# Closing two units at a time, border steps at other times, and a mask in two operations

## The chip, the cores and the metric

One core of a Trainium2 chip runs the whole kernel in one launch. The metric is the time of one launch on the device in microseconds (us), the median of the runs. The engines are named as in the profile: PE is TensorE (PEld its weight loads), DVE is VectorE, ACT is ScalarE, POOL is GpSimd, SP is SyncE, which issues the DMAs.

## What is computed

One decoder layer on x of 1024 tokens by 1024 columns, in float32. One projection feeds two attention groups: a sparse one (8 heads of 64), in which an indexer scores the causal keys and each query keeps its 256 best, and a differential one (4 heads of 128). Their outputs are joined and projected, then an MLP follows; each half has a norm before and after.

```python
def block(i):                     # differential attention, per 128 queries
    p = probs(q1, k1f) - lam * probs(q2, k2f)
    o = jnp.einsum('bhqs,bshe->bqhe', p, vf)
...
o_d = (rmsnorm(o_d, g_diff_sub[layer]).astype(f32) * (1.0 - lam_init)).astype(x.dtype)
...
_, sel = lax.top_k(score, topk)   # sparse attention: 256 keys of each query
...
mix = jnp.concatenate([o_a.reshape(B, S, DSA_W), o_d.reshape(B, S, DIFF_W)], axis=-1)
y = jnp.einsum('bsc,cd->bsd', mix, w_out[layer])
x = x + rmsnorm(y, g_post_mix[layer])
h = rmsnorm(x, g_pre_mlp[layer])
u = jax.nn.relu(jnp.einsum('bsd,df->bsf', h, w_up[layer]))
y = jnp.einsum('bsf,fd->bsd', u * u, w_down[layer])
x = x + rmsnorm(y, g_post_mlp[layer])
```

## The kernel before

Tokens lie in 8 blocks of 128. A float32 factor of a product is split into a high part (a copy in the format fp32r, mostly by ACT) and a low part (the difference, mostly by DVE), and a product is three passes over them; names with `hl`, `hi`, `lo` or a last index 0 and 1 are such parts. The stages, by the trace's time:

- 0 to 200 us: projections of v, of the indexer and its scores (`idx_unit`, tile `si`).
- 200 to some 511: differential attention. A unit is one head and one block, 32 in all. `diff_A` computes both softmaxes (L622 adds the mask and takes the maximum on DVE, L624 the exponential on ACT) and joins them, p = p0 + p1 * st (L671). `diff_groups` transposes p and multiplies it by v into the PSUM bank `od`. `diff_end` (L707 to L716) closes a unit: ACT copies one half of `od` scaled by the reciprocal sum (L710), DVE scales the other half and adds it (L711), ACT squares, POOL takes the root (L103, L106), DVE scales by the root and by g_sub (L715), and a DMA writes the 128x128 result to `mb_d`. Between units PE runs pieces of the projections still due (`pj`, `pv_j`). Beside this runs the search of the 256th score, 31 rounds in two groups of three blocks: ACT counts signs (L523) and DVE one block's (L520), POOL compares (L525, L527), DVE sets bits (L528). At its end `topk_mask1` and `topk_mask2` make a mask of each of six blocks: `te` is 1 where a score is at the threshold, `tu` counts these along the row (L554), and three operations (L564 to L566) join sign and count. Here a scheduler sets the order on the engines; `tc.issue_after` ties steps of the search to units.
- some 473 to 670: sparse attention with these masks as the additive term of its softmax. `outB_load` (L846 to L850) reads `mb_d`, transposes it and splits it for the part of the output projection that is made here (`yb`, L868).
- 670 to 741: the rest of the output projection (`ya`, L1061) and, block by block, both norms (`block`). `load_wo(0)` loads four weight tiles through `split_w` into the two buffers of the tag `wst`.
- 741 to 1071: MLP up, in passes p of seven products P1 to P7 over sums and differences of operand quarters, as `up_mm` (L1023) runs them. `up_weights` makes the weights' sums (`su`) and splits, `mlp_up` adds the products up (`e1`, `e2`, `e3`, `u1`, `u2`), takes relu and square (L1186, L1187), makes sums again (`sd`, L1281 to L1286) and stores parts (`stg`).
- 1071 to 1351: MLP down, units (chunk c, quarter q) of seven products of six matmuls (`down_mm`, L1391); ACT or DVE moves each product to `yu` and `yq` (L1422, L1424). Then `last_unit`, four times, with the last norm (L1516 to L1535).

From 670 on all five engines' orders are written out: every step is put into a list by `do(t, step)` with a due time t in us, and the list is sorted by it. Due times are counted from the start of the block stage: `E` is the end of the last block's products, `U0` is E + 13 (the first pass's reference), `OPEN` E + 14.3, `D0` the start of the down products; `end[p, "P3"]` is a product's planned end, MM = 0.229 a planned matmul. An engine takes its steps in this order, so a step that waits holds all that stand behind it on its engine.

## Time and profile before

| | |
|---|---|
| runs | 1413.58, 1413.93, 1414.21 us; median 1413.93 |
| the profiled execution | 1407.41 us, its span 1405.6 us |
| PE | 1305.7 us busy, 93% of the span, 6520 matmuls |
| DVE | 1113.6 us, 79% |
| ACT | 748.0 us, 53% |
| POOL | 381.3 us, 27% |

Busy times are shares of the whole span and mix stages with different limits; a stretch's own row says which engine is near full there. In rows of single instructions the first number is the start, the second the duration, and the bracket at the end tells how long the engine was idle before it and whose end it waited for. PEclk is the clock that was granted to TensorE, as a share of its full one; on 2.4 GHz as 1.00, 0.50 is 1.2 GHz.

### The profile page before, as it was taken

What the parts mean: (1) busy time and instruction counts of PE and PEld (TensorE: products, weight loads), DVE (VectorE), ACT (ScalarE), POOL (GpSimd) and SP (SyncE); (2) the same over time, 40 slices, a digit from 0 to 9 for tenths busy, and PEclk for the clock granted to TensorE, in tenths of its full rate; (3) what the DMA queues carried; (4) which work ended last, traced back from release to release, by engine and by line L of the source; (5) the groups of instructions that cost most, each with busy time, mean ns of one, the idle gap of its engine ahead of it and who ended that gap; (6) DMA issues with size and microseconds to landing.
All of it is one profiled execution on the core that took longest, in us unless ns stands there. A gap on an engine that the chain in (4) does not pass through costs nothing.

```text
span 1405.6 us, 19947 instructions
## 1 busy us (share of the span) xinstructions
PE 1305.7 (93%) x6520; PEld 1094.3 (78%) x6520; DVE 1113.6 (79%) x2020; ACT 748.0 (53%) x1435; POOL 381.3 (27%) x559
## 2 busy tenths in 40 slices
PE   8999978999998879999788799999998999999997
PEld 8888857778886758888566688888887888888885
DVE  5538969898898888887698788888887578878666
ACT  5305538988974468887454566666666421112112
POOL 5477654775565243332120000000000000000002
PEclk9999998999998979999899899999999999999999
DMA  8766344465554465431661476766778776767646
GB/s 328 257 180 193 108 134 108 130 176 160 157 155 123 118 188 151 137 106 55 230 216 45 165 262 246 255 234 244 254 267 287 261 243 236 261 213 267 224 175 214
DMA packets 152169, 272.89 MB, mean 194 GB/s; under 512 B 15105, under 2 KB 83841, under 8 KB 152065
## 3 DMA queue, kind: packets, MB, share of 16 engines
q1 hardware_dynamic: 152064, 271.61, 58.8%
q8 instruction: 52, 0.85, 0.3%
q14 instruction: 53, 0.43, 0.1%
HBM read 172.46 MB, written 99.09 MB: 193 GB/s over the span
## 4 chain that ended last, share of the span: by engine, by line
PE 60%; DVE 16%; ACT 8%; issue 6%; POOL 5%; DMA 4%; SPq 0%; POOLq 0%; DVEq 0%; ACTq 0%
PE qab L1391 10%; PE pab L1023 8%; PE pj L166 7%; PE qc L1391 6%; PE qd L1391 6%; PE pc L1023 5%; PE pd L1023 5%; PE sa L621 2%; PE pv_j L252 2%; ACT jk L523 2%; PE v L354 2%; PE yb L868 2%; PE oa L825 1%; PE pta L811 1%; DMA v_d_d<-vt 1%
## 5 line engine op out<-in xcount | busy, mean ns | idle before, releaser
L166 PE MATMUL pj<-hT,w_whl 128*128 128x512 f32 (+1 forms) x960 | 226.7, 386 | 4.4 <-DVE vt L230 1.2
L166 PEld LDWEIGHTS pj<-hT,w_whl 128*128 128x128 f32 x960 | 173.7, 190 | 38.4 <-DVE vt L230 1.5
L1527 POOL TENSOR_TENSOR sq<-ss 128x1 f32<-128x1 f32 x8 | 5.6, 699 | 636.8 <-ACT jk L1520 636.8
L523 ACT ACTIVATE jk<-score,vbits 128x768 bf16<-128x768 f32 (+1 forms) x124 | 121.9, 983 | 16.0 <-DVE vbits L528 12.9
L624 ACT ACTIVATE p<-p,st 128x512 f32<-128x512 f32 (+7 forms) x108 | 84.7, 785 | 22.8 <-DVE st L622 18.1
L1023 PE MATMUL pab<-HB,w_up 128*128 128x512 f32 x384 | 92.9, 392 | 0.0
L1023 PEld LDWEIGHTS pab<-HB,w_up 128*128 128x128 f32 x384 | 72.1, 188 | 15.7
L868 PE MATMUL yb<-wo,mbhl 128*128 128x512 f32 x192 | 77.6, 436 | 0.6 <-ACT mbhl L849 0.5
L252 PE MATMUL pv_j<-w_whl,hT 128*128 128x256 f32 x576 | 73.0, 288 | 1.0 <-DVE fm L556 1.0
L252 PEld LDWEIGHTS pv_j<-w_whl,hT 128*128 128x128 f32 x576 | 71.6, 198 | 1.4 <-PE sa L621 1.1
L974 ACT ACTIVATE w_up<-su 128x1024 fp32r<-128x1024 f32 x32 | 33.7, 1052 | 63.1 <-DVE su L1008 59.8
L817 DVE TENSOR_TENSOR ptahl<-pta,ptahl 128x512 fp32r<-128x512 f32 (+2 forms) x112 | 55.4, 495 | 10.7 <-ACT ptahl L816 8.5
L474 DVE SCALAR_TENSOR_TENSOR score<-rl,wsgn,score 128x512 f32<-128x512 f32 (+5 forms) x42 | 54.8, 1305 | 11.0 <-ACT rl L470 8.7
L470 ACT ACTIVATE rl<-si,wabs 128x512 f32<-128x512 f32 (+5 forms) x48 | 40.4, 847 | 43.1 <-PE si L468 33.5
L793 POOL TENSOR_SCALAR p<-p,st 128x128 f32<-128x128 f32 (+7 forms) x60 | 46.8, 784 | 56.5 <-DVE st L792 55.1
L816 ACT ACTIVATE ptahl<-pta 128x512 fp32r<-128x512 f32 (+2 forms) x112 | 49.1, 441 | 22.2 <-PE pta L811 19.1
L1061 PE MATMUL ya<-wo,mixA 128*128 128x512 f32 x192 | 51.8, 426 | 9.8 <-ACT wo L111 4.6
L212 POOL TENSOR_TENSOR mm<-mm 128x512 f32<-128x512 f32 (+1 forms) x40 | 52.6, 1323 | 25.7 <-DVE mm L193 14.5
L1023 PE MATMUL pc<-HT,w_a 128*128 128x512 f32 x192 | 48.9, 406 | 7.8 <-DVE e L1238 7.8
L825 PE MATMUL oa<-ptahl,Va 128*128 128x256 f32 x320 | 53.1, 289 | 3.1 <-DVE ptahl L817 3.0
L621 PE MATMUL sa<-Kd,Qd 128*128 128x512 f32 (+4 forms) x192 | 46.8, 372 | 9.4 <-DVE st L622 9.4
L825 PEld LDWEIGHTS oa<-ptahl,Va 128*128 128x128 f32 x320 | 46.1, 189 | 12.0 <-DVE ptahl L817 4.7
(247 smaller groups left out, 3446.1 us busy)
## 6 DMA issues: line engine op xcount, KB each, us to landing
ul<-u_d SPq DMA_DIRECT2D x56, 896.0 KB, 6.1
u_d<-stg SPq DMA_DIRECT2D x184, 256.0 KB, 2.8
...
```

What stands on the lines that cost most here:

```text
L166: T.matmul(p[:m, :t1 - t0], wv[pw][:, kt, :m], hTs(ph, kt, t0, t1), start=(kt == 0 and j == 0), stop=(kt == KT - 1 and j == 2))
L212: G.tensor_tensor(o, o, mm[half][:, 1, :n], op=op)
L252: T.matmul(p[:, j2 * 256:(j2 + 1) * 256], hTs(ph, kt, tb * P, (tb + 1) * P), w[:, pw, (kt % 4) * 256:(kt % 4 + 1) * 256], start=(kt == 0 a ...
L474: last = V.scalar_tensor_tensor(sc, r[:, :n], wsgn[:, i, h:h + 1], sc, op0=ALU.mult, op1=ALU.add)
L523: A.activation(junk_b()[:, :n], score[i], AF.Sign, bias=t[:, j:j + 1].bitcast(F32), scale=-1.0, accum_out=f[:, j:j + 1])
L621: T.matmul(s[:, b, :c1 - c0], Qd[:, hl0 + part, :], K[:, c0:c1], start=(part == 0), stop=(part == 1))
L624: A.activation(p[:, :n], p[:, :n], AF.Exp, bias=nm, scale=-1.0, accum_out=l)
L817: V.tensor_sub(hl[:, 1, c0:c1], pt[:, c0:c1], hl[:, 0, c0:c1].bitcast(F32))
L825: T.matmul(o[:, :256], v[:, 2 * g2 + kk, :], hl[:, part, kk * 256:(kk + 1) * 256], start=(g2 == 0 and kk == 0 and part == 0), stop=(last a ...
L868: T.matmul(p, hl[:, pm, ct, :], wo[1][pw][ct // 2][:, ct % 2, ch * 512:(ch + 1) * 512], start=(ct == 0 and j == 0), stop=(ct == 3 and j == 2))
L1023: T.matmul(o, w[:, pw, kt, :], H[h][ph][:, kt, :], start=(first and kt == 0 and j == 0), stop=(last and kt == 3 and j == 2), skip_group_ch ...
L1391: T.matmul(o, left[j][:, l, pl, :], right[j][:, pr, :], start=(first and j == 0 and i == 0), stop=(last and j == 1 and i == 2), skip_group ...
```

## The change

1. `diff_end` closes two units together. Each unit's `od`, 256 columns, is copied by ACT without a scale. With the second unit of a pair DVE adds both units' halves in one operation, ACT squares twice, POOL does four operations on 128x2 tiles, DVE scales both units in one operation, and two DMAs follow. The root takes in the softmax's sum, so there is no scaling before it; g_sub becomes one column that `outB_load` applies after the transposition.
2. `topk_mask2` joins sign and count by one sum, 4096 * sign + count, and makes the mask by one comparison.
3. `load_wo(0)` loads weight tiles 2 and 3 into buffers of the tag `mbhl`.
4. From E to U0: the last block's normalisation, product of x and its weight, and transposes go in halves, and due times of weights' splits and of u1 move.
5. Around D0: due times of the last pass's relus, squares and stores, of `wd_z`'s low parts and of the pool's closing move later.
6. `last_unit`: the four sums take banks ab0, qc, ab1, qd in place of ab0, ab1, qc, qd, and the root's first half is made early.
7. Four small tiles move to other pools, g_sub's load reads a column.

```diff
@@ topk_mask2
-        V.tensor_scalar(s_, s_, 0.0, MASK, op0=ALU.is_ge, op1=ALU.mult)
-        V.scalar_tensor_tensor(u_, u_, f[:, 2:3], e_, op0=ALU.is_le, op1=ALU.mult)
-        V.scalar_tensor_tensor(score[i], u_, -MASK, s_, op0=ALU.mult, op1=ALU.add)
+        V.scalar_tensor_tensor(u_, s_, 4.0 * S, u_, op0=ALU.mult, op1=ALU.add)
+        V.tensor_scalar(score[i], u_, f[:, 2:3], MASK, op0=ALU.is_gt, op1=ALU.mult)
...
@@ diff_end
-        ot = at.tile([P, 2, P], F32, tag="ot", bufs=2, name="ot")
-        A.activation(ot[:, 0, :], o[:, P:2 * P], AF.Copy, scale=st[:, 4:5])
-        V.scalar_tensor_tensor(ot[:, 1, :], o[:, :P], st[:, 4:5], ot[:, 0, :], op0=ALU.mult, op1=ALU.add)
-        ss = sm.tile([P, 1], F32, name="ssd")
-        A.activation(ot[:, 0, :], ot[:, 1, :], AF.Square, accum_out=ss)
-        r = rstd_of(ss, 2 * HD)
-        V.scalar_tensor_tensor(ot[:, 1, :], ot[:, 1, :], r, g_sub, op0=ALU.mult, op1=ALU.mult)
-        ld.dma_start(mb_d[i * P:(i + 1) * P, h * P:(h + 1) * P], ot[:, 1, :])
+        u = box["u"]
+        if u == 0:
+            duo["o"] = at.tile([P, 2, 2, P], F32, tag="ot", bufs=2, name="ot")
+        ot = duo["o"]
+        A.activation(ot[:, u].rearrange("p a d -> p (a d)"), o[:, :256], AF.Copy)
+        if u == 0:
+            duo["i"] = i
+            return
+        V.tensor_add(ot[:, :, 0, :], ot[:, :, 0, :], ot[:, :, 1, :])
+        ss = sm.tile([P, 2], F32, name="ssd")
+        for k in range(2):
+            A.activation(ot[:, k, 1, :], ot[:, k, 0, :], AF.Square, accum_out=ss[:, k:k + 1])
...
+        G.tensor_tensor(l2, box["l"], box["l"], op=ALU.mult)
+        G.tensor_scalar(m, ss, 1.0 / (2 * HD * EPS), 1.0, op0=ALU.mult, op1=ALU.mult)
+        G.tensor_add(m, m, l2)
+        G.tensor_tensor(m, m, mhalf2, op=ALU.pow)
+        V.tensor_mul(ot[:, :, 0, :], ot[:, :, 0, :], m[:, :, None].to_broadcast([P, 2, P]))
+        for k, b in enumerate((duo["i"], i)):
+            ld.dma_start(mb_d[b * P:(b + 1) * P, h * P:(h + 1) * P], ot[:, k, 0, :])
...
@@ outB_load
-        A.activation(hl[:, 0, :], pt, AF.Copy)
-        V.tensor_sub(hl[:, 1, :], pt, hl[:, 0, :].bitcast(F32))
+        A.activation(hl[:, 0, :], pt, AF.Copy, scale=g_sub)
+        V.scalar_tensor_tensor(hl[:, 1, :], pt, g_sub, hl[:, 0, :].bitcast(F32), op0=ALU.mult, op1=ALU.subtract)
...
@@ load_wo
+            raw_in = {} if half or ct < 2 else dict(pool=p2, tag="mbhl")
...
@@ block, last one
+                do(t + 13.8 + 0.65 * k, normed, cs(k))
+                do(tt - 0.6 + 0.6 * k, tr, (k,))
...
@@ mlp_up
-        t11 = max(end[p, "P2"] + 1.05, OPEN + 0.1 if p == 0 else end[p - 1, "P3"] + 3.5)
+        t11 = max(end[p, "P2"] + 1.05, OPEN + 6.2 if p == 0 else end[p - 1, "P3"] + 3.5)
...
+        final = p == NP - 1
+        do(end[p, "P3"] + (2.9 if final else 1.2), lambda: relu2(a21(), a21()))
+        do(end[p, "P4"] + (4.2 if final else 0.65), lambda: relu2(a12(), a12()))
...
@@ last_unit
-            b["o"] = ab[:, 0, :], ab[:, 1, :], psM("qc"), psM("qd")
+            b["o"] = ab[:, 0, :], psM("qc"), ab[:, 1, :], psM("qd")
...
-                G.tensor_add(s, x["ss"][:, 0:1], x["ss"][:, 1:2])
-                x["r"] = rstd_of(s, D)
+                G.tensor_scalar(x["m"][:, 1:2], x["ss"][:, 1:2], 1.0 / D, x["m"][:, 0:1], op0=ALU.mult, op1=ALU.add)
+                G.tensor_tensor(x["r"], x["m"][:, 1:2], mhalf, op=ALU.pow)
```

Where instructions stand in a row now, at three places. On SP, at the end of the sparse attention, the kernel before has its last stores of `yb`, the reads for the first block and the two last loads of the output weights (`wst<-in_wo`) in this order (lines of the changed kernel are shifted):

```order
L874 DMA yb_d<-yt 128x512 x3
L1029 DMA g_post<-in_g_post_mix 128x1024
L1050 DMA y_8142<-yb_d 128x1024 x2
L132 DMA wst<-in_wo 128x1024
L874 DMA yb_d<-yt 128x512
L132 DMA wst<-in_wo 128x1024
L970 DMA wst<-in_wu 128x1024 x2
```

On SP at the same place, the changed kernel has:

```order
L899 DMA yb_d<-yt 128x512
L134 DMA wst<-in_wo 128x1024
L899 DMA yb_d<-yt 128x512 x2
L1054 DMA g_post<-in_g_post_mix 128x1024
L1075 DMA y_8058<-yb_d 128x1024 x2
L134 DMA wst<-in_wo 128x1024
L995 DMA wst<-in_wu 128x1024 x2
L899 DMA yb_d<-yt 128x512
```

The third load stands ahead of three stores now, and the fourth ahead of the last one. On DVE, before the second pass of the up products (`e` is the sum on which its third product waits, `su` the sums of weights of the pass after, `sd` sums of u, `w_up` and `stg` low parts), before:

```order
L1006 TENSOR_TENSOR su<-wst 128x512
L1234 TENSOR_TENSOR e_8979<-pab,e_8756 128x512
L1007 TENSOR_TENSOR su<-wst 128x512
L1008 TENSOR_TENSOR su<-su,wst 128x512
L1009 TENSOR_TENSOR su<-wst,su 128x512
L1281 TENSOR_TENSOR sd<-u_8903 128x512
L1284 TENSOR_TENSOR sd<-sd,u_8836 128x512
L1285 TENSOR_TENSOR sd<-u_8836,u_8903 128x512
L1286 TENSOR_TENSOR sd<-u_8836,sd 128x512
L977 TENSOR_TENSOR w_up<-wst,w_up 128x1024
L1264 TENSOR_TENSOR stg<-sd,stg 128x8x128
L1238 TENSOR_TENSOR e_9017<-pc,e_8979 128x512
```

The same engine at the same place in the changed kernel:

```order
L1267 TENSOR_TENSOR e_8894<-pab,e_8672 128x512
L1315 TENSOR_TENSOR sd<-u_8820 128x512
L1318 TENSOR_TENSOR sd<-sd,u_8800 128x512
L1319 TENSOR_TENSOR sd<-u_8800,u_8820 128x512
L1320 TENSOR_TENSOR sd<-u_8800,sd 128x512
L1031 TENSOR_TENSOR su<-wst 128x512
L1032 TENSOR_TENSOR su<-wst 128x512
L1033 TENSOR_TENSOR su<-su,wst 128x512
L1034 TENSOR_TENSOR su<-wst,su 128x512
L1002 TENSOR_TENSOR w_up<-wst,w_up 128x1024
L1298 TENSOR_TENSOR stg<-sd,stg 128x8x128
L1271 TENSOR_TENSOR e_8934<-pc,e_8894 128x512
```

The four sums `sd` stand ahead of the four sums `su`, and the first `e` ahead of both. On ACT at the start of the down products (`wd_z` and `wd_b` are splits of weights, `u` a relu or a square, `stg` a stored part, `yu` and `yq` the evictions of the products), before:

```order
L974 ACTIVATE wd_z<-wst_11085 128x1024
L1186 ACTIVATE u_11284<-u_11284 128x512
L1187 ACTIVATE u_11284<-u_11284 128x512
L1260 ACTIVATE stg<-u_11284 128x8x128
L1186 ACTIVATE u_11257<-u_11257 128x512
L1187 ACTIVATE u_11257<-u_11257 128x512
L1422 ACTIVATE yu<-qab 128x512
L1260 ACTIVATE stg<-u_11257 128x8x128
L1422 ACTIVATE yq_11327<-qc 128x512
L974 ACTIVATE wd_b<-wst 128x512
```

The same engine at the same place in the changed kernel:

```order
L999 ACTIVATE wd_z<-wst_11002 128x1024
L1456 ACTIVATE yu<-qab 128x512
L1219 ACTIVATE u_11201<-u_11201 128x512
L1220 ACTIVATE u_11201<-u_11201 128x512
L1456 ACTIVATE yq_11239<-qc 128x512
L1219 ACTIVATE u_11174<-u_11174 128x512
L1220 ACTIVATE u_11174<-u_11174 128x512
L1294 ACTIVATE stg<-u_11201 128x8x128
L999 ACTIVATE wd_b<-wst 128x512
L1294 ACTIVATE stg<-u_11174 128x8x128
L1456 ACTIVATE yq_11239<-qab 128x512
```

The eviction `yu` stands right behind the split of `wd_z`, and the relus, squares and stores of the last pass behind it.

## Rows read from the trace of the kernel before

**Rows 1.** Table of stretches, times in us from the span's start

```profile
core 0: us, PE busy (x) PEld busy (x) DVE busy (x) ACT busy (x) POOL busy (x), PEclk, DMA share, GB/s
200.00:420.00 220.00, 200.91 (x1126) 173.99 (x1125) 199.41 (x525) 181.48 (x428) 136.73 (x234) 0.96 0.53 148
420.00:520.00 100.00, 77.76 (x452) 67.14 (x450) 87.62 (x202) 51.12 (x129) 46.66 (x59) 0.83 0.52 148
800.00:1000.00 200.00, 200.00 (x875) 164.14 (x875) 168.89 (x217) 127.03 (x176) 0.00 (x0) 1.00 0.70 245
1080.40:1087.40 7.00, 7.00 (x18) 5.54 (x19) 3.72 (x5) 3.37 (x5) 0.00 (x0) 0.57 0.94 349
794.68:799.80 5.12, 5.12 (x12) 4.09 (x13) 2.72 (x3) 1.89 (x3) 0.00 (x0) 0.51 1.01 369
```

**Rows 2.** Waits of PE: us in total, times, longest

```profile
PE sa L621 <- DVE st L622: 12.9, 10, 3.2
...
PE od L700 <- DVE ot L711: 1.8, 1, 1.8
```

**Rows 3.** Groups by line: count | busy us, mean ns | idle before it

```profile
L710 ACT ACTIVATE ot<-od,st 128x128 f32<-128x128 f32 x32 | 11.4, 356 | 10.7 <-PE od L700 9.6 <-DMA mb_d<-ot 1.1
...
L711 DVE SCALAR_TENSOR_TENSOR ot<-od,st,ot 128x128 f32<-128x128 f32 x32 | 10.9, 342 | 1.9 <-ACT ot L710 1.9
...
L715 DVE SCALAR_TENSOR_TENSOR ot<-ot,rs_r,g_sub 128x128 f32<-128x128 f32 x32 | 14.4, 451 | 2.4 <-POOL rs_r L106 2.2
...
L837 DVE TENSOR_TENSOR ota<-oa,ota 64x256 f32<-64x256 f32 x32 | 13.4, 420 | 3.0 <-ACT ota L836 2.1
```

**Rows 4.** Groups by line: the mask's three operations, and the scores' scaling

```profile
L564 DVE TENSOR_SCALAR te<-te 128x512 bf16<-128x512 bf16 (+5 forms) x6 | 3.0, 505 | 0.0
...
L565 DVE SCALAR_TENSOR_TENSOR tu<-tu,fm,te 128x512 f32<-128x512 f32 (+5 forms) x6 | 6.1, 1022 | 0.1
...
L566 DVE SCALAR_TENSOR_TENSOR score<-tu,te 128x512 f32<-128x512 f32 (+5 forms) x6 | 5.3, 880 | 0.0
...
L472 DVE TENSOR_SCALAR score<-rl,wsgn 128x512 f32<-128x512 f32 (+5 forms) x6 | 4.6, 761 | 0.0
```

**Rows 5.** Order of time, loads of the output weights

```profile
670.48 0.33 SPq L132 DMA_DIRECT2D wst<-in_wo  x1
...
675.33 1.06 ACT L111 ACTIVATE wo<-wst 128x1024 fp32r<-128x1024 f32 x1 [4.22 <-DMA wst<-in_wo]
...
676.43 3.89 PE L1061 MATMUL ya<-wo,mixA 128*128 128x512 f32 x6 [4.62 <-ACT wo L111]
```

**Rows 6.** Order of time, from the last block to the second pass up

```profile
752.51 1.28 DVE L1107 SCALAR_TENSOR_TENSOR y<-xt,rs_r,g_mlp 128x1024 f32<-128x1024 f32 x1
...
758.72 4.76 PE L1023 MATMUL pab<-HT,w_up 128*128 128x512 f32 x12 [3.73 <-ACT HT L1144]
...
768.53 4.38 PE L1023 MATMUL pd<-HT,w_up 128*128 128x512 f32 x11 [1.07 <-DVE HT L1145]
...
786.69 0.68 DVE L1281 TENSOR_TENSOR sd<-u 128x512 f32<-128x512 f32 x1
...
789.34 0.60 ACT L1186 ACTIVATE u<-pab 128x512 f32<-128x512 f32 x1 [5.85 <-DVE sd L1286]
...
794.68 5.30 PE L1023 MATMUL pc<-HT,w_a 128*128 128x512 f32 x12 [7.81 <-DVE e L1238]
```

**Rows 7.** Order of time, first step of the down products

```profile
1073.36 1.04 ACT L974 ACTIVATE wd_z<-wst 128x1024 fp32r<-128x1024 f32 x1
...
1079.77 0.58 ACT L1422 ACTIVATE yu<-qab 128x512 f32<-128x512 f32 x1
...
1080.40 2.93 PE L1391 MATMUL qab<-wd_x,ul 128*128 128x512 f32 x6 [3.74 <-ACT yu L1422]
```

**Rows 8.** Order of time, the tail

```profile
1393.01 2.95 PE L1391 MATMUL qd<-wd_p,ul 128*128 128x512 f32 x12
...
1398.11 0.68 DVE L1516 TENSOR_TENSOR yq<-qd,yq 128x512 f32<-128x512 f32 x1
...
1399.68 0.70 POOL L1527 TENSOR_TENSOR sq<-ss 128x1 f32<-128x1 f32 x1 [3.54 <-ACT jk L1520]
```

More of the change, by code (lines that the diff above doesn't have):

```diff
@@ L97, in hybrid_block @@
     V.memset(mhalf, -0.5)
+    mhalf2 = cst.tile([P, 2], F32, name="mhalf2")
+    V.memset(mhalf2, -0.5)
     gt = lambda name: wp.tile([P, D], F32, tag="g", bufs=1, name=name)
@@ L128, in hi_next, with split_w @@
         cp(next(hi_eng), o, i)
-    def split_w(src, dst_hi, dst_lo, hi, lo_eng=V):
-        st = wp.tile([P, D], F32, tag="wst", bufs=2, name="wst")
+    def split_w(src, dst_hi, dst_lo, hi, lo_eng=V, pool=wp, tag="wst"):
+        st = pool.tile([P, D], F32, tag=tag, bufs=2, name="wst")
         ld.dma_start(st, src)
@@ L357, in hybrid_block @@
     csk = at.tile([P, NB, 2, HD], F32, tag="vt", bufs=3, name="csk")
-    widx = cst.tile([P, NB, 8], F32, name="widx")
+    widx = at.tile([P, NB, 8], F32, tag="qd", bufs=3, name="widx")
     mk_ = rope_mm("mmk").rearrange("p a (b c) -> p a b c", c=HD)
@@ L597, in hybrid_block @@
         steps += seqs[0][k:k + 1] + seqs[1][k:k + 1]
-    lam4 = cst.tile([P, 4, HD], F32, name="lam4")
+    lam4 = at.tile([P, 4, HD], F32, tag="ot", bufs=2, name="lam4")
     for j, nm in enumerate(("lambda_q1", "lambda_k1", "lambda_q2", "lambda_k2")):
@@ L610, in hybrid_block @@
     V.tensor_scalar(neglam, neglam, -LAM_INIT, None, op0=ALU.add)
-    g_sub = cst.tile([P, P], F32, name="g_sub")
-    ld.dma_start(g_sub, bcast_rows(a["g_diff_sub"], P))
-    V.tensor_scalar(g_sub, g_sub, 1.0 - LAM_INIT, None, op0=ALU.mult)
+    g_sub = cst.tile([P, 1], F32, name="g_sub")
+    g_col = a["g_diff_sub"]
+    ld.dma_start(g_sub, bass.AP(tensor=g_col.tensor, offset=g_col.offset, ap=[[1, P], [1, 1]]))
+    V.tensor_scalar(g_sub, g_sub, (1.0 - LAM_INIT) * EPS ** -0.5, None, op0=ALU.mult)
     def softmax_num(Qd, hl0, K, mask, n, p, nm, l):
@@ L1087, in add_x, with tr @@
             ld.dma_start(x1_d[row, :], b["x"])
-        def tr():
-            for k in range(2):
+        def tr(ks):
+            for k in ks:
                 b["t", k] = psM("tr")
@@ L1106, in block, with normed @@
         do(t + 12.4, rs2)
-        do(t + 13.8, lambda: V.scalar_tensor_tensor(b["y"], b["x"], b["r2"], g_mlp, op0=ALU.mult, op1=ALU.mult))
+        def normed(c):
+            V.scalar_tensor_tensor(b["y"][:, c], b["x"][:, c], b["r2"], g_mlp[:, c], op0=ALU.mult, op1=ALU.mult)
         tt = t + (15.2 if fin else 20.7)
-        do(tt, tr)
+        if pos < NB - 1:
+            do(t + 13.8, normed, slice(0, D))
+            do(tt, tr, (0, 1))
+        else:
+            for k in range(2):
+                do(t + 13.8 + 0.65 * k, normed, cs(k))
+                do(tt - 0.6 + 0.6 * k, tr, (k,))
         cols = slice(q * P, (q + 1) * P)
@@ L1131, in block @@
             do(e + (0.7 if fin else 1.0), lambda: V.tensor_sub(T2(), b["t", 1], T1()))
-            do(e + 0.8, lambda: A.activation(H["B22"][0][:, :, cols], ps4(1), AF.Copy))
+            do(e + (1.9 if end else 0.8), lambda: A.activation(H["B22"][0][:, :, cols], ps4(1), AF.Copy))
             do(e + (2.0 if fin else 4.0), lambda: V.tensor_sub(T3(), T2(), bb[q][:, 0, :]))
@@ L1272, in mlp_up @@
         if plain:
-            store(lambda: b["u1"], 0, z - 0.85, z + 0.6)
-            store(lambda: b["u2"], 2, z + 2.3, z + 3.4)
+            store(lambda: b["u1"], 0, z + (3.0 if final else -0.85), z + (4.6 if final else 0.6))
+            store(lambda: b["u2"], 2, z + (3.6 if final else 2.3), z + (4.9 if final else 3.4))
         else:
@@ L1525, in rs, with rs0 @@
             def rs(x=x):
-                s = sm.tile([P, 1], F32, name="sq")
-                G.tensor_add(s, x["ss"][:, 0:1], x["ss"][:, 1:2])
-                x["r"] = rstd_of(s, D)
+                x["r"] = sm.tile([P, 1], F32, name="rs_r")
+                G.tensor_scalar(x["m"][:, 1:2], x["ss"][:, 1:2], 1.0 / D, x["m"][:, 0:1], op0=ALU.mult, op1=ALU.add)
+                G.tensor_tensor(x["r"], x["m"][:, 1:2], mhalf, op=ALU.pow)
+            def rs0(x=x):
+                x["m"] = sm.tile([P, 2], F32, name="rs_2")
+                G.tensor_scalar(x["m"][:, 0:1], x["ss"][:, 0:1], 1.0 / D, EPS, op0=ALU.mult, op1=ALU.add)
+            do(e - SUM + 1.6, rs0)
             do(e + 1.6, rs)
```

35 lines of the change are left out of this document (20 added, 15 removed).

## The prediction

> **What bounds the kernel now.** TensorE and VectorE are the two busy engines, and a gain has to come from the time in which TensorE (PE) stands; so I read the table of stretches first, stage by stage [rows 1]. From 800 to 1000 us PE is busy 200.00 of 200: 875 matmuls, 0.2286 us each at the full clock. Nothing that frees another engine helps there. From 200 to 420 PE lacks 19.1 us, while VectorE is busy 199.4 of 220. From 420 to 520 PE lacks 22.2 of 100, VectorE is busy 87.6, ACT 51 and POOL 47. So in these two stretches VectorE is the engine that sets the pace, most clearly in the second. The list of waits agrees: PE's largest one is on VectorE's softmax line, 12.9 us, whereas the closing step that the change rewrites made PE wait only 1.8 [rows 2]. The remaining idle time of PE lies at the borders between stages, each with one late step that can be named: the loads of the output weights, the last block ahead of the MLP, the first step of the down products, the tail.
>
> The profiled execution took 1407.41 us (span 1405.6), 6.5 less than the median 1413.93. What lies between them is not in the trace; I make the sum on the profiled one and carry it over one to one.
>
> **Closing two units at once.** Removed on VectorE: 32 additions from PSUM of 342 ns and 32 scalings of 451 ns on average [rows 3], 10.9 + 14.4 = 25.3 us. Added: 16 additions and 16 multiplications of 128x256. The nearest row is a 256-wide addition of 420 ns [rows 3], so 32 x 0.42 = 13.4, a saving of 11.9 us. That addition reads one operand from PSUM; the new ones read both from SBUF. The removed scaling also read both from SBUF, and it averages 451 against 342 for the removed addition of the same size, 1.32 times as long. If the new operations stretch as much, they cost 17.7 and the saving is 7.6. ACT copies 256 columns where it copied 128 in 356 ns [rows 3]; a copy of 512 columns out of PSUM takes 0.58 [rows 7], so some 0.43, 32 x 0.07 = 2.4 us more on an engine that is half idle where it matters. POOL gets 64 small operations for 64: nothing either way.
>
> **The mask.** Three operations on each of six blocks took 3.0 + 6.1 + 5.3 = 14.4 us [rows 4]. The new pair is one three-operand operation like the last of the three, 5.3, and one comparison in float32; the only row of such a shape is the scaling of the scores, 761 ns on average at the same six widths [rows 4], 4.6 together. Saving 4.5; if the comparison costs what the bf16 one did (3.0), 6.1; I take 5.5. The bounds are 8.3 (the whole bf16 line, and half of the last) and nothing.
>
> A rule speaks against both savings. The trace shows the stretched mean of 451 named above. The Trainium skill, "SBUF — State Buffer", section "Who interferes with whom", says that a VectorE instruction with two SBUF inputs, or a one-input one in a two-port mode, blocks a GpSimd instruction that reads SBUF and is blocked by it, for the whole instruction. The stretched mean agrees with that. By this rule the new additions, whose removed forms read PSUM, and the float32 comparison join those that can be blocked: the closing saves 7.6 and the mask may save nothing.
>
> **What of it reaches the end.** With 23 of the 32 closings before 420, VectorE loses 5.5 to 8.6 us there and 2.1 to 3.4 plus the mask's 5.5 after, 13 to 17.5 in all. It is only time where VectorE is what PE waits for. Before 420 PE is 91% busy and ACT 82% [rows 1], so once VectorE is earlier these are next: I take 2 of the 7. After 420 nothing else is near full, and the blocks that follow wait for the masks: 4.5 of the 8.3. **Middle: 6.5**, bounds 0 (or a loss, below) and 17.5.
>
> **Loads of the output weights.** Today SP issues the third load at 670.48, when a buffer comes free; ACT splits it at 675.33 and PE stands 4.62 us until 676.43 [rows 5]. The changed kernel puts loads three and four into other buffers; the third stands ahead of the last stores in SP's order, and the fourth behind the last matmul before this stage, near 669.6. With 4.85 us from issue to split as in the row, the fourth lands near 674.5 and is split by 675.6; now the fourth split ends at 678.3. The split of the third no longer waits. **2.8** (1 to 4; SP passes two stores and two reads, 0.3 each, beside the load).
>
> **Last block ahead of the MLP.** VectorE normalises the block in one step at 752.51, 1.28 us; the transposes follow at 753.93, the first difference's copies on ACT end the chain and PE starts at 758.72 after 3.73 us [rows 6]. In halves, the first transpose starts 0.65 sooner, and two low parts of weights, which stood on VectorE between the transposes and the differences, come after them: the copy is ready near 756.6, 2.1 sooner. The next start, 768.53, waits for low parts behind ACT's eight copies, and ACT no longer evicts u ahead of them: near 765.8. Then PE stands 7.81 us until 794.68; before it, ACT's eviction of u waits 5.85 until 789.34 for the last sd step, behind four su steps [rows 6]. In the new order sd stands ahead of su, each four steps of 0.68, and ACT's split of w_up ahead of u. With PE 2.5 earlier by then, sd ends at 789.3 - 2.5 - 2.7 = 784.1; su follows to 786.8, the low parts of w_up and stg, twice as wide and 1.2 each, to 789.2, and the sum e on which PE waits to 789.9, 4.8 sooner than 794.68. PE's wait stays, somewhat shorter, and so does the lower clock behind it: 12 matmuls at a granted clock of 0.51 [rows 1], the lower level of 1.2 GHz, in 5.30 us where the full rate gives 2.74. **4.5** (2 to 6).
>
> **First step of the down products.** PE waits 3.74 us, to 1080.40, for the eviction yu at 1079.77, which stands on ACT behind the last pass's relus, squares and a store, though the split of wd_z had ended at 1074.40 [rows 7]. The next 18 matmuls took 7.0 us at a mean granted clock of 0.57 [rows 1], where the full rate gives 18 x 0.2286 = 4.1: 2.9 more. In the new order yu stands right behind the split of wd_z; qab is complete by then, so it is done near 1075. PE goes on at 1080.40 - 3.74 = 1076.66 without a wait or loss of clock: 3.74 + 2.9, less 0.3 for one later eviction. Next late could be the low part of the second wd_z, which the fifth group of products needs; VectorE makes it right behind its split on ACT, before that group's turn. **6.3** (3 if a new wait drops the clock again, to 6.6).
>
> **Tail.** The last unit's first add waits for both halves of a bank pair, 24 matmuls, and the later ones queue behind it: the last add starts at 1398.11, although PE's last matmul ended at 1393.01 + 2.95 = 1395.96 [rows 8]. With the pair's halves apart in the order, the first add follows after 12 matmuls and the last follows PE, near 1396.0: 2.1. POOL's sum, 0.70 us on the final chain [rows 8], goes: 2.8, and one read less: **2.9** (1.5 to 3.2). The moved lambda and g_sub loads: 0, give or take 0.5, hidden behind the projections; the eight outB low parts change form at the same width: 0.
>
> **Sum.** 2.8 + 4.5 + 6.3 + 2.9 = 16.5 at the borders, 6.5 in the middle: 23.0. The profiled execution would take 1384.4, the median 1413.9 - 23.0 = 1390.9, **1391 us**.
>
> **The rivals.**
> - The middle gives nothing: the scheduler makes a new order there, ACT and POOL carry the rounds of the top-256 search, and PE waits on the same softmax line for other reasons. For it: ACT at 82% before 420; against it: 420 to 520, where only VectorE is near full. Borders alone: 1413.9 - 16.5 = 1397.
> - VectorE and GpSimd block each other more: the closing saves 7.6, the mask nothing, 10 us become 7.6 of VectorE and perhaps 2.5 of time: 1395. This is what the rule of the skill's page named above would do; the rows bear out the stretch but not who caused it.
> - The middle is wholly bound by VectorE: 16 to 17 us come back, 1413.9 - 16.5 - 16.5 = 1381. Against it: PE's 91% before 420.
> - The change doesn't do at the borders what it says: a wait takes the place of yu at the down products (low part of wd_z), and u's eviction meets su's tile. Left are the tail, the output weights and 2 or 3 us: some 8 us, 1406; with the middle lost against it as well, 1413.
> - Slower: one ot tile now spans two units and only ACT's copy releases the bank od. If that copy has to wait for the stores of a pair two before, PE's next products wait with it. It decides from 16.5 / 16 = 1.03 us per pair; at 1.5 us it costs 24, 1421. Against it: PE waited 1.8 us on the closing in all [rows 2].
>
> **How the numbers follow.** The forecast, 1391 with 1387 to 1396 of its own: 0.45. Middle nothing, 1397: 0.22. Blocking, 1395: 0.08. Middle whole, 1381: 0.12. Borders fail: 0.08, of which 0.03 still faster and 0.05 no change. Closing holds the banks, 1421: 0.05. A difference under 0.2%, 2.8 us, can't be told from none. Faster: 0.45 + 0.22 + 0.08 + 0.12 + 0.03 = 0.90; same 0.05; slower 0.05. The range reaches from the whole middle with a little more from the borders, 1379, to 1404, where borders partly fail; outside lie some 0.15.
>
> **What would show it.** In the new trace: ya's third group without a wait near 672 to 675; PE at 100% through the first down unit at the full clock; the last add within half a microsecond of the last matmul; a stall of 5 to 6 us before the second pass of the up products. In the middle, VectorE's busy time down by 13 to 17 us from 200 to 520, and the start of the stage after it 5 to 8 earlier. Wrong it would be if that stage starts no earlier, if pair additions take over 0.6 us, or if PE waits for the bank od.

## The result, and the profile after

The changed kernel takes 1382.57 us in the median (1381.15 to 1383.30) beside 1413.78 of the kernel before: ratio 0.9778, 95% interval 0.9761 to 0.9795, 31.2 us less. In the profiled executions the gain is 25.1 us (span 1380.5 after 1405.6). It was forecast at 1391, in a range of 1379 to 1404: the time lies in the range, 8 us below the forecast, and two terms of the sum, the middle and the down products, came out quite differently.

Where the time went, by the starts of the first and last matmuls of each stage (first profile of either kernel; times in us; the last `qab` is here the last one that reads `wd_b`, ahead of the four last units):

| stretch | before | after | change | forecast |
|---|---|---|---|---|
| start to the last indexer product (si) | 193.8 | 198.5 | +4.7 | 0 |
| from there to the first yb: differential attention | 313.6 | 294.0 | -19.6 | } -6.5 |
| first yb to first ya: sparse attention | 162.0 | 164.9 | +2.9 | } |
| first ya to first product up | 71.5 | 66.5 | -5.0 | -2.8 |
| up | 330.8 | 325.2 | -5.6 | -4.5 |
| down, to the last qab | 271.2 | 271.4 | +0.2 | -6.3 |
| last qab to the end | 62.7 | 60.0 | -2.7 | -2.9 |

The 2.9 us more between the first `yb` and the first `ya` come back in all six profiles with the whole change (164.3 to 165.8, where the kernels without it have 160.9 to 163.5); no run explains them.

The table of stretches after, to be held against [rows 1]: VectorE is a little busier than it was in the same times, and more gets done in them (1161 matmuls for 1126, 516 for 452).

```profile
core 0: us, PE busy (x) PEld busy (x) DVE busy (x) ACT busy (x) POOL busy (x), PEclk, DMA share, GB/s
200.00:420.00 220.00, 205.72 (x1161) 177.87 (x1160) 203.47 (x507) 183.87 (x435) 140.83 (x240) 0.97 0.56 158
420.00:520.00 100.00, 81.95 (x516) 72.62 (x515) 88.78 (x213) 58.44 (x143) 47.27 (x60) 0.90 0.52 152
```

Some of PE's longest waits after. The wait on softmax has shrunk from 12.9 to 7.3 us [rows 2], the wait for e from 7.81 to 5.5 [rows 6]; the wait of 3.74 us for yu [rows 7] is gone, but one of 1.3 stands later in the stage, and the waits for the loads ul, 0.4 us before, have grown to 3.5:

```profile
PE sa L624 <- DVE st L625: 7.3, 7, 3.0
...
PE pc L1048 <- DVE e L1271: 5.5, 1, 5.5
...
PE qab L1425 <- DMA ul<-u_d: 3.5, 3, 2.1
...
PE pab L1048 <- ACT HT L1177: 2.0, 1, 2.0
...
PE qab L1425 <- ACT yu L1456: 1.3, 1, 1.3
```

The closings and the mask after, groups by line as in [rows 3, 4]. L723 is ACT's copy, L727 and L737 are VectorE's two operations on pairs, L567 and L568 the mask:

```profile
L723 ACT ACTIVATE ot<-od 128x256 f32<-128x256 f32 x32 | 11.8, 370 | 4.1 <-PE od L709 4.1
...
L727 DVE TENSOR_TENSOR ot<-ot 128x256 f32<-128x256 f32 x16 | 11.7, 731 | 0.4 <-ACT ot L723 0.4
...
L737 DVE TENSOR_TENSOR ot<-ot,rd_m 128x256 f32<-128x256 f32 x16 | 7.3, 457 | 1.7 <-POOL rd_m L736 1.7
...
L567 DVE SCALAR_TENSOR_TENSOR tu<-te,tu 128x512 f32<-128x512 bf16 (+5 forms) x6 | 5.3, 881 | 0.0
...
L568 DVE TENSOR_SCALAR score<-tu,fm 128x512 f32<-128x512 f32 (+5 forms) x6 | 4.5, 745 | 0.0
```

VectorE's work on closings fell from 25.3 to 11.7 + 7.3 = 19.0 us, on the mask from 14.4 to 5.3 + 4.5 = 9.8: 10.9 us in all, for 16.7 us of time in the two attention stages. That is more than was taken away, and it is what the experiments had to explain first.

The borders after, in order of time. Output weights (compare [rows 5], a wait of 4.62): PE's waits here are 0.75 and 0.64.

```profile
660.75 0.73 PE L1086 MATMUL ya<-wo,mixA 128*128 128x512 f32 x2 [0.75 <-DVE wo L137]
...
661.01 1.06 ACT L113 ACTIVATE wo<-wst 128x1024 fp32r<-128x1024 f32 x1 [1.07 <-DMA wst<-in_wo]
...
662.12 0.51 PE L1086 MATMUL ya<-wo,mixA 128*128 128x512 f32 x1 [0.64 <-ACT wo L113]
```

Last block and second pass up (compare [rows 6]): 2.00 for 3.73, 0.80 for 1.07, ACT's wait on sd 2.37 for 5.85, PE's stall 5.45 for 7.81, still followed by 12 matmuls in 5.46.

```profile
739.71 0.50 PE L1048 MATMUL pab<-HT,w_up 128*128 128x512 f32 x1 [2.00 <-ACT HT L1177]
...
748.60 2.79 PE L1048 MATMUL pd<-HT,w_up 128*128 128x512 f32 x11 [0.80 <-DVE HT L1178]
...
766.87 0.60 ACT L1219 ACTIVATE u<-pab 128x512 f32<-128x512 f32 x1 [2.37 <-DVE sd L1320]
...
772.39 5.46 PE L1048 MATMUL pc<-HT,w_a 128*128 128x512 f32 x12 [5.45 <-DVE e L1271]
```

Tail (compare [rows 8]): the last add begins 0.03 us after the last matmul, where it began 2.15 after; POOL's first operation on the chain takes 0.68 for 0.70.

```profile
1370.24 2.92 PE L1425 MATMUL qd<-wd_p,ul 128*128 128x512 f32 x12
...
1373.19 0.69 DVE L1550 TENSOR_TENSOR yq<-qd,yq 128x512 f32<-128x512 f32 x1
...
1374.87 0.68 POOL L1561 TENSOR_SCALAR rs<-ss,rs 128x1 f32<-128x1 f32 x1 [2.37 <-ACT jk L1554]
```

### The profile page after: what moved, and what is told of

It is laid out like the page before. It is cut to its first block, busy times and chain, and to the rows that moved or that the text cites. A ratio compares the mean times of both kernels' runs of the same rounds, so it can differ in the third digit from the quotient of the medians.

```text
span 1380.5 us, 19876 instructions
## 1 busy us (share of the span) xinstructions
PE 1298.5 (94%) x6520; PEld 1088.3 (79%) x6520; DVE 1105.1 (80%) x1984; ACT 748.5 (54%) x1435; POOL 384.2 (28%) x559
## 4 chain that ended last, share of the span: by engine, by line
PE 51%; DVE 17%; ACT 8%; issue 5%; POOL 4%; DMA 2%; SPq 1%; DVEq 0%; POOLq 0%; ACTq 0%
PE qab L1425 10%; PE pab L1048 8%; PE qc L1425 6%; PE qd L1425 6%; PE pc L1048 6%; PE pd L1048 5%; ACT jk L525 3%; PE sa L624 2%; DVE p L625 2%; PE yb L893 2%; PE pj L168 2%; PE oa L850 2%; ACT p L627 1%; PE pta L836 1%; DVE ptahl L842 1%
## 5 line engine op out<-in xcount | busy, mean ns | idle before, releaser
L1566 POOL TENSOR_SCALAR rs<-ss 128x1 f32<-128x1 f32 x8 | 3.9, 490 | 608.4 <-ACT jk L1554 608.4
L254 PE MATMUL pv_j<-w_whl,hT 128*128 128x256 f32 x576 | 69.6, 280 | 3.5 <-POOL f L527 1.8
L254 PEld LDWEIGHTS pv_j<-w_whl,hT 128*128 128x128 f32 x576 | 67.6, 188 | 5.2 <-POOL f L527 2.0
L217 POOL TENSOR_TENSOR hl<-mm,hl 128x512 fp32r<-128x512 f32 (+1 forms) x40 | 56.8, 1428 | 0.7
```

What stands on the lines that cost most here:

```text
L217: G.tensor_sub(hl[:, 1, :n], o, hl[:, 0, :n].bitcast(F32))
L254: T.matmul(p[:, j2 * 256:(j2 + 1) * 256], hTs(ph, kt, tb * P, (tb + 1) * P), w[:, pw, (kt % 4) * 256:(kt % 4 + 1) * 256], start=(kt == 0 a ...
```

## The experiments

Medians stand beside those of the kernel before, run between them on the same chip: 1411.48 (the first four kernels), 1411.02 (the four of the changed kernel's first unit down) and 1410.47 (the rest). Three theories on the middle run through several texts: W, time follows the work taken from VectorE; R, it is the release of the bank and the closing's chain; O, any new order of the scheduler moves the stage.

**The kernel before, again.** No edit.

> The kernel before, unchanged, once more with a profile. The profiled execution of before took 1407.41 us (span 1405.6) and its timed runs 1413.6 to 1414.2; in the changed kernel the two agree to 0.3 us. Theory P: the 6.4 us belong to that one execution, and a new profile of the same kernel has a span near 1412, with one more wait or a lower granted clock at a place that can be named. Rival Q: the profile always runs faster than the timed runs of this kernel, and the span is again near 1405.6.

Measured: 1410.78 in the median of ten executions, from 1407.93 to 1415.17; the profiled one took 1410.18 (span 1408.3). Neither theory: single executions of this kernel scatter over 7 us, and the profile of 1407.41 that I worked from was one at the low end. The stage lengths of the two profiles agree within 0.4 us behind the first 196 us. So the 6.5 us between profile and median were scatter between executions, not a term of the sum.

**The paired closings alone.**

```diff
-        V.scalar_tensor_tensor(ot[:, 1, :], o[:, :P], st[:, 4:5], ot[:, 0, :], op0=ALU.mult, op1=ALU.add)
...
+        A.activation(ot[:, u].rearrange("p a d -> p (a d)"), o[:, :256], AF.Copy)
+        if u == 0:
+            duo["i"] = i
+            return
+        V.tensor_add(ot[:, :, 0, :], ot[:, :, 0, :], ot[:, :, 1, :])
...
```

> Before, with the paired closings alone (and the small tiles' moves and the g_sub column that they need). Theory W (work): the differential stage is paced by VectorE, and time follows the work taken from it; the closings took 25.3 us of VectorE before and 19.0 after, so 6.3 us less work gives at most 6 us: 1408 or more. Theory R (release and order): the stage gains more than the work, since the od bank and the closing's chain no longer pass through VectorE, and the clock recovers with fewer waits: 1400 to 1404. Rival N: the closings give nothing alone, 1412 to 1415.

Measured: 1397.47, ratio 0.9896 (0.9881 to 0.9911), 14.0 us less (12.6 to 16.8). That is over twice what theory W allows, and at the far end of theory R, whose 1400 was 13.8 below the 1413.78 known then.

**The mask alone.**

```diff
-        V.tensor_scalar(s_, s_, 0.0, MASK, op0=ALU.is_ge, op1=ALU.mult)
-        V.scalar_tensor_tensor(u_, u_, f[:, 2:3], e_, op0=ALU.is_le, op1=ALU.mult)
-        V.scalar_tensor_tensor(score[i], u_, -MASK, s_, op0=ALU.mult, op1=ALU.add)
+        V.scalar_tensor_tensor(u_, s_, 4.0 * S, u_, op0=ALU.mult, op1=ALU.add)
+        V.tensor_scalar(score[i], u_, f[:, 2:3], MASK, op0=ALU.is_gt, op1=ALU.mult)
```

> Before, with the two-operation mask alone. The three operations took 14.4 us of VectorE, the two in the changed kernel 9.8, so 4.6 less. Theory W: up to 4.6 us, 1409 to 1411. Theory R: what matters are the closings, the mask gives 0 to 2, 1412 to 1414.

Measured: 1402.80, ratio 0.9946 (0.9924 to 0.9967), 8.7 us less (4.7 to 10.7): more than both theories, though the interval nearly reaches the 4.6 of theory W.

**All borders alone.**

```diff
+            raw_in = {} if half or ct < 2 else dict(pool=p2, tag="mbhl")
...
+                do(t + 13.8 + 0.65 * k, normed, cs(k))
...
+        do(end[p, "P3"] + (2.9 if final else 1.2), lambda: relu2(a21(), a21()))
...
+            b["o"] = ab[:, 0, :], psM("qc"), ab[:, 1, :], psM("qd")
```

> Before, with all edits at the borders alone (loads of the output weights, last block, down products, tail), without closings and mask. By the changed kernel's trace the four borders gave 4.8, 5.7, -0.2 and 2.7 us: 13.0 in all, 1400.8. By the prediction 16.5: 1397.3. If the borders only gain because the stage ahead of them changed, under 9: above 1405.

Measured: 1399.83, ratio 0.9913 (0.9898 to 0.9927), 11.7 us less (10.3 to 14.4): near the 13.0 from the changed kernel's trace, and clear of the 9 under which the borders would hang on the stage ahead of them. By stages beside the repeated kernel before: ya 71.1 to 68.1, up 330.8 to 324.8, down 271.4 to 272.0, tail 62.7 to 60.4. Beside the old middle the borders gain as they do in the changed kernel, and the down products gain nothing here either.

**The bank released by ACT.** The sum of the two halves is made from SBUF, one unit at a time.

```diff
-        A.activation(ot[:, 0, :], o[:, P:2 * P], AF.Copy, scale=st[:, 4:5])
-        V.scalar_tensor_tensor(ot[:, 1, :], o[:, :P], st[:, 4:5], ot[:, 0, :], op0=ALU.mult, op1=ALU.add)
+        A.activation(ot.rearrange("p a d -> p (a d)"), o[:, :256], AF.Copy, scale=st[:, 4:5])
+        V.tensor_add(ot[:, 1, :], ot[:, 1, :], ot[:, 0, :])
```

> Before, with one thing changed in the closing: ACT copies all 256 columns of the bank od, scaled, so the bank is free when ACT is done, and VectorE adds the two halves from SBUF; still one unit at a time, the same number of operations. The paired closings alone gave 14 us. Theory R (release): most of it comes from the bank being free earlier; 5 us or more here, under 1406. Theory W or O (work and order): the release is worth 0 to 2 us, 1409 to 1412.

Measured: 1407.25, ratio 0.9968 (0.9950 to 0.9987), 3.2 us less (1.8 to 7.1), between the two expectations. No operation of VectorE is removed, so this is not work.

**The mask, with 3.0 of the 4.6 us of removed work given back.**

```diff
         V.tensor_scalar(score[i], u_, f[:, 2:3], MASK, op0=ALU.is_gt, op1=ALU.mult)
+        V.tensor_scalar(s_, s_, 0.0, MASK, op0=ALU.is_ge, op1=ALU.mult)
```

> Before, with the two-operation mask and behind it, per block, one more operation of VectorE on the sign's tile, whose result nobody reads, as long as the removed one (3.0 us in the six). So 1.6 of the 4.6 us of removed work stay removed, and the mask is still ready two operations earlier. The mask alone gave 8.7 us. Theory W (work): 1.6/4.6 of it, some 3: 1408.5. Theory M (the mask is ready sooner): 6 us or more, 1402 to 1405. Theory O (the scheduler's order): anything from 1400 to 1412, with the third block's scan either close behind its threshold's step, as in the mask alone, or 8 us behind it, as before.

Measured: 1407.22, ratio 0.9974 (0.9954 to 0.9994): 3.2 us less than before (0.8 to 6.5), where the mask alone gave 8.7. The added operations, 3.0 us of work, put back 5.5 us between the medians and 3.9 in the stretch of the two profiles below. That is what theory W forecast (some 3 us left); theory M's 6 us or more lies at the far end of the interval.

**Two small tiles in other pools.**

```diff
-    widx = cst.tile([P, NB, 8], F32, name="widx")
+    widx = at.tile([P, NB, 8], F32, tag="qd", bufs=3, name="widx")
-    lam4 = cst.tile([P, 4, HD], F32, name="lam4")
+    lam4 = at.tile([P, 4, HD], F32, tag="ot", bufs=2, name="lam4")
```

> Before, with only the two small tiles widx and lam4 in other pools: no work is taken away. It changes when their loads may start and with that the scheduler's order. Theory W: 0, 1411 give or take 1.5. Theory O (a new order alone moves the stage by several us): 3 us or more either way.

Measured: 1409.16, ratio 0.9988 (0.9969 to 1.0007): no difference that can be told. This one new start of loads, with nothing taken away, does not give what the other edits gave; no other was tried. These two are the only small tiles whose pool the change alters; point 7 of the change counts four.

**What these seven say together.** The same stretch, from the last si to the first yb, in each (columns of the view: stretch, then busy time of PE, PEld, DVE, ACT, POOL, the granted clock, DMA). Before, repeated:

```profile
196.20:510.20 314.00, 274.20 (x1549) 237.48 (x1547) 280.69 (x702) 225.99 (x535) 180.91 (x287) 0.93 0.52 150
```

Bank released by ACT:

```profile
197.50:504.80 307.30, 268.76 (x1550) 233.50 (x1548) 281.81 (x702) 229.96 (x536) 184.79 (x287) 0.94 0.54 151
```

Paired closings:

```profile
197.10:496.60 299.50, 270.41 (x1549) 236.00 (x1547) 276.57 (x672) 225.93 (x533) 181.48 (x286) 0.93 0.55 155
```

Mask:

```profile
196.60:502.20 305.60, 270.68 (x1549) 235.47 (x1548) 273.88 (x696) 225.72 (x536) 179.43 (x287) 0.94 0.53 152
```

Changed kernel:

```profile
198.50:492.50 294.00, 265.41 (x1550) 231.24 (x1548) 270.07 (x664) 225.78 (x534) 177.68 (x284) 0.96 0.55 157
```

| kernel | stretch | VectorE busy | VectorE idle |
|---|---|---|---|
| before, repeated | 314.0 | 280.7 | 33.3 |
| tiles in other pools | 312.5 | 280.0 | 32.5 |
| mask, work given back | 309.5 | 277.0 | 32.5 |
| bank released by ACT | 307.3 | 281.8 | 25.5 |
| mask alone | 305.6 | 273.9 | 31.7 |
| pairs alone | 299.5 | 276.6 | 22.9 |
| changed kernel | 294.0 | 270.1 | 23.9 |

Single profiles can be compared here, because this stretch scatters little: it took 313.5 to 314.0 us in the three profiles with the old middle (before, its repeat, the borders alone) and 293.5 to 296.8 in the six with the whole change. In other stages they scatter more: the last si lies anywhere between 193.8 and 198.8, and the profile of the mask with work given back has 336.2 us in the up products, which its edit doesn't touch, for 330.8.

The mask takes 6.8 us off VectorE's busy time and 1.6 off its idle time, 8.4 in all. The mask's own rows in this stretch fell by 3.2; the rest of the 6.8 lies in operations that the edit does not touch, and why they became shorter was not found. The paired closings take 4.1 off the busy time (the operation that sets the search's bits, L528, took 20.3 us there for 17.3, against the saving) and 10.4 off the idle time. The release alone takes 7.8 off the idle time. One wait on ACT shrinks together with it. Before, repeated, in the same stretch (us in total, times, longest):

```profile
ACT ot L713 <- DVE ot L711: 15.0, 9, 5.6
```

Bank released by ACT:

```profile
ACT ot L713 <- DVE ot L711: 6.0, 9, 1.3
```

Paired closings:

```profile
ACT ot L730 <- DVE ot L727: 1.8, 4, 0.8
```

Mask:

```profile
ACT ot L713 <- DVE ot L711: 5.4, 7, 1.2
```

Before, ACT's square of a closing waited for VectorE's addition, 15.0 us in nine times, up to 5.6 at once, and what stood behind it on ACT, exponentials and sign counts among it, waited too. With the release by ACT this wait is 6.0 us in all, in pairs 1.8, and VectorE's idle time is 7.8 and 10.4 shorter. But the mask's run speaks against this wait as the cause: there it fell as far, to 5.4, and VectorE's idle time only by 1.6. Sorted by the engine that VectorE waited for, its waits in this stretch were, before, 11.3 us on ACT and 10.5 on PE; with the release 7.6 and 5.0, in pairs 8.0 and 5.0, with the mask 13.9 and 11.3. The two largest of its waits for PE before, repeated:

```profile
DVE mm L193 <- PE pj L166: 2.0, 1, 2.0
DVE pthl L117 <- PE ptd L689: 1.9, 2, 1.7
```

The second is gone in both edits to the closings; of the first 1.1 is left in pairs and none with the release. So the two edits to the closings take away waits of VectorE for PE and ACT, and the mask doesn't. Which step of a closing carries that is not shown.

By these runs the 14.0 us of the paired closings are, as an estimate, 4.1 to 6.3 of removed work, 3.2 of release, and 4.5 to 6.7 that no run isolates: theory R holds in part. For the mask theory W fits best, with a size that the removed work doesn't explain, and theory O gave nothing in the one case that was tried. The parts overlap: alone they gave 14.0 + 8.7 + 11.7 = 34.4 us, the whole change 31.2 in the result and 27.7 in the run below.

**The down products, four ways.** The changed kernel, once more, as the measure:

> The changed kernel, unchanged, on the chip of the next three, as their measure. 1380 to 1384, with the down products' first matmul to last in 271.4 us as in its first profile.

Measured: 1383.33, ratio 0.9802 (0.9778 to 0.9825); first to last qab 274.2 us, outside the 271.4 that I expected.

The edits at the start of the down products undone:

```diff
-        do(end[p, "P3"] + (2.9 if final else 1.2), lambda: relu2(a21(), a21()))
+        do(end[p, "P3"] + 1.2, lambda: relu2(a21(), a21()))
...
-            store(lambda: b["u2"], 2, z + (3.6 if final else 2.3), z + (4.9 if final else 3.4))
+            store(lambda: b["u2"], 2, z + 2.3, z + 3.4)
...
```

> The changed kernel with the edits at the start of the down products undone (the last pass's relus, squares and stores, the low parts of wd_z and the pool's closing at their old times). The prediction gave these edits 6.3 us; if that holds, the time is 6 us above the changed kernel. Theory L: they take away the first wait (3.74 us and the lower clock behind it), but the loads ul of the third unit, behind the later stores in SP's order, give it all back; undone, the time is within 1 us of the changed kernel, and the first down unit shows the wait of 3.7 us for yu again.

Measured: 1381.93, ratio 0.9788 (0.9767 to 0.9809): 1.4 us faster than the changed kernel beside it, within the scatter of the two. The prediction's 6.3 us are not there. The first unit has its wait of 3.9 us for yu again, and first to last qab take 270.0.

The stores behind the loads ul:

```diff
-                for q in range(4):
-                    ld.dma_start(u_d[p // 2, q, :, p % 2, g:g + n], st[:, q].bitcast(F32))
...
+            if final:
+                do(D0 + 42 * MM + 0.08, dmas)
```

> The changed kernel with one thing moved: the last pass's eight stores are issued by SP behind the third unit's loads ul, not ahead of them (the loads go out when the first unit ends, near 1059.7 on the changed kernel's clock, where they went out at 1065.8). Theory L: PE's waits for ul (2.06 and 1.25 us) and the lower clock behind them go, 3 to 5 us faster than the changed kernel; the wait of 1.28 us for yu stays. Rival D: the loads are late because the DMA queues are full there; then the waits stay and the time is within 1 us of the changed kernel's.

Measured: 1383.85, ratio 0.9804 (0.9789 to 0.9819): no gain, so theory L names the wait and not the cause. The loads go out at 1057.55 and PE no longer waits for them in the third unit; in their place PE waits 5.15 for yu. So neither expectation came as written: the waits for ul went, and the time stayed.

And VectorE's low parts earlier:

```diff
-            store(lambda: b["u1"], 0, z + (3.0 if final else -0.85), z + (4.6 if final else 0.6))
-            store(lambda: b["u2"], 2, z + (3.6 if final else 2.3), z + (4.9 if final else 3.4))
+            store(lambda: b["u1"], 0, z + (3.0 if final else -0.85), z + (4.2 if final else 0.6))
+            store(lambda: b["u2"], 2, z + (3.6 if final else 2.3), z + (4.3 if final else 3.4))
```

> As the run before, and VectorE makes the two low parts of the stores ahead of the weights' differences of the next chunk (due times 4.2 and 4.3 for 4.6 and 4.9), so that ACT can split wd_x 1.3 us sooner. If the wait of 1.28 us for yu hangs on that, another 1 to 1.5 us: 5 to 6 us faster than the changed kernel, the whole 6.3 of the prediction. If not, the same as the run before.

Measured: 1381.93, ratio 0.9794 (0.9779 to 0.9809): the wait of 1.28 us went as expected, but the one for yu stayed at 4.74, and the time is that of the run before within the scatter.

The stores behind the next loads of weights as well:

```diff
-                do(D0 + 42 * MM + 0.08, dmas)
+                do(D0 + 14.2, dmas)
```

> The changed kernel with the last pass's eight stores issued by SP behind the third unit's loads ul and also behind the next two loads of weights (wd), and VectorE's two low parts of the stores at 4.2 and 4.3. With the stores behind ul alone, PE waited 5.15 us for yu instead, because the weights' loads went out at 1068.3, landed near 1075, and VectorE and ACT stood behind them. Theory S: what costs the gain is whatever stands behind the eight stores in SP's order; with both loads ahead, neither wait appears, the down products' first matmul to last takes 267 to 269 us (271.4 to 275.4 in the runs of the changed kernel so far) and the time is 1376 to 1380. Rival H: the stores hold their tiles longer, and a wait for a tile takes their place: 1382 or more.

Measured: 1381.95, ratio 0.9786 (0.9751 to 0.9821). Theory S fell, rival H came: PE waits 3.71 us for yu.

How the gain is lost, in order of time. The changed kernel: yu is evicted behind the split of wd_z and PE goes on without the wait, as forecast; then SP issues eight stores, and behind them the loads for which PE stands:

```profile
1050.83 1.04 ACT L999 ACTIVATE wd_z<-wst 128x1024 fp32r<-128x1024 f32 x1
...
1051.78 0.58 ACT L1456 ACTIVATE yu<-qab 128x512 f32<-128x512 f32 x1
...
1053.73 1.56 PE L1425 MATMUL qab<-wd_x,ul 128*128 128x512 f32 x6
...
1060.53 4.45 SPq L1300 DMA_DIRECT2D u_d<-stg  x8
...
1065.77 1.10 SPq L1419 DMA_DIRECT2D ul<-u_d  x2
...
1073.00 0.96 PE L1425 MATMUL qab<-wd_b,ul 128*128 128x512 f32 x3 [2.06 <-DMA ul<-u_d]
...
1075.20 1.41 PE L1425 MATMUL qab<-wd_b,ul 128*128 128x512 f32 x3 [1.25 <-DMA ul<-u_d]
```

With the loads ahead of the stores, the weights' loads behind them were late, VectorE and ACT stood in line, and yu with them:

```profile
1068.26 2.41 SPq L995 DMA_DIRECT2D wst<-in_wd  x2
...
1075.38 0.69 DVE L1398 TENSOR_TENSOR wst<-wst 128x512 f32<-128x512 f32 x1 [6.77 <-DMA wst<-in_wd]
...
1076.10 1.06 ACT L999 ACTIVATE wd_y<-wst 128x1024 fp32r<-128x1024 f32 x1 [8.85 <-DVE wst L1398]
...
1078.67 1.65 PE L1432 MATMUL qab<-wd_x,ul 128*128 128x512 f32 x3 [5.15 <-ACT yu L1463]
```

With both ahead, the stores held the tile into which ACT was to write the next weights:

```profile
1068.58 5.93 SPq L1305 DMA_DIRECT2D u_d<-stg  x8
...
1076.07 1.06 ACT L999 ACTIVATE wd_y<-wst 128x1024 fp32r<-128x1024 f32 x1 [7.40 <-DMA u_d<-stg]
...
1078.64 2.92 PE L1432 MATMUL qab<-wd_x,ul 128*128 128x512 f32 x6 [3.71 <-ACT yu L1463]
```

Windows of 10 us, the first three from the first down product on. The changed kernel:

```profile
1049.10:1059.10 10.00, 9.79 (x41) 7.37 (x40) 6.70 (x10) 8.91 (x14) 0.00 (x0) 1.00 0.75 284
1059.10:1069.10 10.00, 8.72 (x38) 6.85 (x37) 8.84 (x11) 6.13 (x9) 0.00 (x0) 1.00 0.80 260
1069.10:1079.10 10.00, 6.69 (x21) 4.72 (x21) 3.06 (x5) 1.83 (x3) 0.00 (x0) 0.83 1.01 410
```

The edits undone:

```profile
1050.60:1060.60 10.00, 5.80 (x23) 4.18 (x22) 5.97 (x8) 7.98 (x12) 0.00 (x0) 0.97 0.88 310
1060.60:1070.60 10.00, 10.00 (x39) 8.00 (x39) 8.39 (x11) 6.55 (x11) 0.00 (x0) 0.86 0.96 349
1070.60:1080.60 10.00, 10.00 (x45) 8.13 (x44) 4.89 (x7) 3.93 (x7) 0.00 (x0) 1.00 0.84 307
```

The first window of the changed kernel is as forecast, 9.79 us of PE at the full clock for 5.80; the third gives it back. There the DMA engines are busy all the time (1.01) while PE has 6.69 of 10 us at a granted clock of 0.83. Over the three windows PE does 100 matmuls in the changed kernel and 107 with the edits undone, and the DMA engines move nearly the same, 9.5 and 9.7 MB by the rates in the rows. In the three variants with the stores moved, the third window has a DMA share of 0.97 to 0.99 and PE works 5.3 to 6.3 us of it. So PE began the second unit 5.5 us earlier (10.4 us behind the first product for 15.9), came to a stretch in which stores, weights and ul were still to be moved, and waited there for whichever SP had put last. Whether the transfers are the limit or only go out too late stays open: four orders with the same time suggest the first, but in the changed kernel the DMA share was only 0.75 and 0.80 in the two windows ahead. An order with fewer bytes in the stretch, or with its transfers spread evenly, was not tried.

## Why the prediction was right, and where it was not

- **What bounds.** Borne out: between 200 and 520 us VectorE sets the pace; work given back to it there cost time again (3.9 us in the stretch for 3.0).
- **Work removed.** The closings saved 6.3 us, below my lower bound of 7.6; the additions took 731 ns on average against 420 from the row I chose, over the 0.6 us that I had named as a sign of being wrong. The stretch that I used as the bound, 1.32 times, was too small: it was 1.7 for the additions, and the last section shows POOL in it. The mask saved 4.6 for 5.5; my bound of 8.3 is both lines whole (3.0 + 5.3), with half of the last it is 5.7.
- **What of it reaches the end: the step that failed.** I took 6.5 of 13 to 17.5, because PE was 91% busy before 420. The two stages gave 16.7 (19.6 less 2.9). Two mistakes: PE at 91% behind a VectorE at 91% was no second limit here; and my sum had only work in it. The 10.4 us of idle time that the pairs took from VectorE had no term; the trace of before has them as VectorE's waits for PE and ACT. Two of my signs show it: VectorE's busy time between the last si and the first yb fell by 9.8 us (279.9 to 270.1), not by 13 to 17, and yet the next stage began 14.9 earlier (507.4 to 492.5), not 5 to 8. The rival that gave the middle its full size, 1381, was the nearest, for a reason that it didn't have: less work went than it supposed.
- **The rivals on blocking and on the bank.** The closings' saving of 6.3 is near the 7.6 of the rival on blocking; its mask, saving nothing, and its time, 1395, did not come. The rival at 1421 fell: ACT's copy waited only for PE (4.1 us), no longer for stores, where it waited 1.1 for them before [rows 3].
- **Output weights.** 2.8 forecast; 5.0 between the first profiles of the two kernels, 2.4 between the second ones, 3.0 with the borders alone. The mechanism was right: of PE's wait of 4.62 there are 0.75 + 0.64 left.
- **Last block.** 4.5 forecast, 5.6 to 6.5 measured; a stall of 5.45 before the second pass and the lower clock behind it stayed, as said.
- **Down products: the other step that failed.** 6.3 forecast, 0 measured. The wait for yu and the lower clock behind it went, as worked out, and the second unit began 5.5 us earlier; but I followed the eviction alone and not the eight stores and their place in SP's order. Next late were ul, weights or tiles, and none of the three orders tried got the time back.
- **Tail.** 2.9 forecast, 2.7 measured, 2.1 of it from the add that follows PE at once. The 0.70 that I gave to POOL did not go: a first operation of 0.68 still stands on the final chain.
- **Moved small loads.** Forecast 0. The first profile lost 4.7 us before the last si; over all profiles this point lies at 193.8 to 197.5 in kernels without the whole change and at 195.1 to 198.8 in those with it, so at most some 1 us is the edit's. It was not settled.
- **Total.** In the two profiles the gain is 25.1 us, near the 23.0 of the sum, and that is luck: the middle gave 10 more than said, the down products 6 and the start 5 less. The medians lie 31.2 apart because the profile of before lay 6.4 below its median and that of after 0.3; to carry the profile's gain over one to one was a third miss. In the later run of the changed kernel the gain was 27.7.
